# Sampled tokens of the state space part: small tiles, a gate and norm of their own, and other places for their eight steps

## The chip, the cores and the metric

The kernel runs on one core of a Trainium2 chip. Its time is device microseconds (us) of one execution, lower is better. Matrix products run on TensorE (PE), elementwise work on VectorE (DVE), ScalarE (ACT, which also evaluates functions) and GpSimd (POOL); SyncE (SP) issues nearly all DMAs, in one queue. All engines run their own instruction queues in order and wait for each other by semaphores.

## What is computed

One layer of a decoder for two groups of requests that share all weights: a prompt of 1024 positions, and 8 sampled tokens that continue from given states. Cut to what matters here:

```python
h = rmsnorm(x, w['norm1_w'])
proj = h @ w['w_in']
q_r, f_r, i_r, g_r, z, xbc_r, dt_r = jnp.split(proj, splits, axis=-1)
# group A: HGRN2 recurrence on q, f, i, g (8 heads of 128) -> o_a
xbc, buf_s_new = causal_dwconv(xbc_r, buf_s, w['ssm_conv_w'], w['ssm_conv_b'])
xbc = jax.nn.silu(xbc)
xs, Bm, Cm = jnp.split(xbc, [D_SSM, D_SSM + SSM_GROUPS * SSM_STATE], axis=-1)
y, S_s_new = ssd_scan(X * dt[..., None], A * dt, Bh, Ch, S_s)   # X: 16 heads of 64
y = y + w['ssm_d'][:, None] * X
y = y.reshape(Bsz, L, D_SSM) * jax.nn.silu(z)
y = rmsnorm(y.reshape(Bsz, L, SSM_GROUPS, -1), w['ssm_norm_w'].reshape(SSM_GROUPS, -1))
x = x + jnp.concatenate([o_a, y], axis=-1) @ w['w_out']
# then norm, gated MLP with a depthwise convolution, residual, final norm
```

For a sampled token the scan is one step: the state of each head is decayed by exp(A dt), the outer product of X dt and B is added, the product of the new state with C, summed over the 128 state columns, is y. The new states are outputs. Width of the state space part is 1024, in 2 groups of 512; all data are float32, and each operand of a large product is split into a high and a low part, so that it takes three matmuls.

## The kernel before, in words

Activations lie feature by token: a tile has 128 features as partitions and 1032 columns, 1024 prompt positions and then the 8 sampled tokens. The input projection is a list of jobs (`in_job`, L290), one for each 128 columns of `w_in`. A job makes three chunks of 344 columns, 72 matmuls in all, in three PSUM banks that rotate; after each chunk `evict` takes the bank over, on ACT. The jobs' order around the change is x0 to x3, x9, x11, x4 to x7 (the tiles of X; 8 to 11 are B and C), z0 to z3, f0, q0, v0, sg0 (head 0 of group A), z4 to z7, f1 and so on. A job's weights are fetched two jobs ahead (`wload`, L180) into two raw and two split buffers; `fetch` (L172) puts a DMA on SP's queue behind the last weight load that the program text had reached.

PE's order is written out by hand. `drive` (L266) runs a stream of larger work, such as the scan `ssd(g)` (L713) of group g, and between its pieces as many job steps (one matmul each) as keep both going; `ssd(0)` runs beside x9 to x7, `ssd(1)` beside z0 to v0, head 0 beside f1 to sg1. `after(n, work)` (L229) emits work n steps later. On the other engines a planner in the compiler orders the instructions, by their place in the program text and by when it believes them ready, so work of a later job may run earlier where its inputs and buffers are there.

`xbc_close` (L363) takes the convolution (four passes, `conv_tail`) and SiLU of one tile; L369 is the prompt's SiLU and L370 that of the sampled tokens, into columns 1024 to 1031 of the same tile. `ssd_front` (L530) and `ssd_back` (L560) do one chunk of 128 positions of the scan: L541/L542 the decays on ACT, L554/L557 the operands on DVE, L574, L580, L590, L593 outputs and state on DVE, L555/L579 on POOL.

`ssm_decode(g, i)` (L625) is one sampled-token step, for tile j = 4g + i (two heads, all 8 tokens). In two halves of 4 tokens it fetches B and C broadcast to 128 partitions and the states (tiles Bb, Cb in tag "d" with 4 buffers, Sd in tag "ld" with 2), decays the states on ACT (L638, four), multiplies B by X dt (L639) and adds (L640) on DVE, writes the state out (L641), multiplies by C on POOL (L642) and sums on DVE (L643); L629 and L644 frame it on 8 columns. It reads and writes columns 1024 to 1031 of X's tile. Its eight calls stand at the begin of x5, x7, z0 and z1 (group 0) and z4 to z7 (group 1).

`ssm_gate(g)` (L653) makes the gate: each z chunk goes through SiLU on ACT (L670, tile sz, tag "z" with 4 buffers), multiplies X in place on DVE (L671), is squared on ACT (L673/L675) and added up (L676). After the group's fourth job and 36 or 50 more steps, `rstd(c)` sums the squares over features with a matmul with ones (bank tag "nx", one buffer, which head 0's L834/L842 use too) and takes the reciprocal root (`rstd_of`, L646: one ACT, three DVE). `tail` then scales the four tiles on DVE (L694) and writes them to the scratch `mix_d`, from which the output projection reads them much later.

Of the kernel before, what the change touches and what calls it, by code (L numbers as in the profile page):

```python
# [8 lines left out]
F32 = mybir.dt.float32  # L9
F32R = mybir.dt.float32r  # L10
U8 = mybir.dt.uint8
AF = mybir.ActivationFunctionType
ALU = mybir.AluOpType
# [3 lines left out]
P = 128  # L17
DM = 1024
T = 1024
ND = 8  # L20
NT = T + ND
CH = 344
NCH = 3
# [27 lines left out]
def hybrid_layer(  # L51
# [9 lines left out]
    V, A, G, PE, SP = nc.vector, nc.scalar, nc.gpsimd, nc.tensor, nc.sync  # L61
# [9 lines left out]
    def nm(s):  # L71
        cnt[0] += 1
        return f"{s}_{cnt[0]}"
# [4 lines left out]
    const = part.enter_context(tc.tile_pool(name="const", bufs=1, side="right"))  # L78
    small = part.enter_context(tc.tile_pool(name="small", bufs=2, side="right"))
    tmp = part.enter_context(tc.tile_pool(name="tmp", bufs=1, side="right"))  # L80

    def tl(tag, name, dt=F32):
        w, n = TAGS[tag]
        return (work if tag in ("hT", "big", "e", "g") else tmp).tile([P, w], dt, tag=tag, bufs=n, name=nm(name))
# [4 lines left out]
    def bank(s, tag="mx"):  # L89
        return psmx.tile([P, 512], F32, tag=tag, bufs=NBANK[tag], name=nm(s))  # L90

    def mm(out, lhsT, rhs, start=True, stop=True):
        PE.matmul(out, lhsT, rhs, start=start, stop=stop)  # L93
# [55 lines left out]
    def col(name, i=0):  # L149
        c = vlay[name] + i  # L150
        return vcol[:, c:c + 1]
# [58 lines left out]
    chunks = [slice(c * CH, (c + 1) * CH) for c in range(NCH)]  # L210
# [18 lines left out]
    def after(n, work):  # L229

        later.append([n, work])
# [106 lines left out]
    Xg = [[None] * 4 for _ in range(2)]  # L338
    BT, CT, S = [None, None], [None, None], [None, None]
    last11 = const.tile([P, XT, 11], F32, name="last11")  # L340
    mix_d = dram.tile([16, P, NT], F32, name="mix_d")
    bc_d = dram.tile([4, ND, P], F32, name="bc_d")

    def conv_tail(acc, ext, nw, wname, bname, j, ntile, n):
        A.activation(acc[:, :n], ext[:, :n], AF.Identity, bias=col(bname, j), scale=col(wname, j))
        for q in range(1, nw):
            V.scalar_tensor_tensor(acc[:, :n], ext[:, q:q + n], col(wname, q * ntile + j), acc[:, :n],
                                   op0=ALU.mult, op1=ALU.add)

    def xbc_open():  # L350
        ext = tl("e", "ext")
        G.memset(ext[:, 0:3], 0.0)
        return ext

    def xbc_evict(j, ext, c, cs, ps):
        e = min(cs.stop, T)
        A.copy(ext[:, 3 + cs.start:3 + e], ps[:, :e - cs.start])
        if c == 2:
            V.tensor_copy(ext[:, 3 + T:3 + T + 32].rearrange("p (b r) -> p b r", r=4)[:, :, 3:4],
                          ps[:, T - cs.start:].unsqueeze(2))  # L360
            V.tensor_copy(last11[:, j, :], ps[:, CH - 11:])

    def xbc_close(j, ext):  # L363
        G.tensor_copy(ext[:, 3 + T:3 + T + 32].rearrange("p (b r) -> p b r", r=4)[:, :, 0:3],
                      bufT[:, j, :].rearrange("p (b r) -> p b r", r=3))
        n = T + 32
        acc = tl("big", "xbc")
        conv_tail(acc, ext, 4, "cw", "cb", j, XT, n)
        A.activation(acc[:, :T], acc[:, :T], AF.Silu)  # L369
        A.activation(acc[:, T:NT], acc[:, T + 3:T + 32:4], AF.Silu)  # L370
        return acc

    def xbc_job(j, put):
        ext = []
        def begin():
            ext.append(xbc_open())
            if j in (5, 7):
                ssm_decode(0, (5, 7).index(j))

        in_job(f"x{j}", OFF_X + j * P, lambda c, cs, ps: xbc_evict(j, ext[0], c, cs, ps), begin=begin, end=lambda: put(xbc_close(j, ext[0])))  # L380

# [20 lines left out]
    ones = keep.tile([P, P], F32, name="ones")  # L402
# [24 lines left out]
    for c, cs in enumerate(chunks):  # L427
        ps = psmm.tile([P, 512], F32, tag="mm", name=nm("dt"))
# [9 lines left out]
    for i in range(9):  # L438
        n = P if i < 8 else ND
# [171 lines left out]
    def d4(t):  # L611
        return t.rearrange("p (b n) -> p b n", n=P)
# [12 lines left out]
    def ssm_decode(g, i):  # L625
        j = g * 4 + i
        xdd = small.tile([P, 2, ND], F32, tag="xdd", name=nm("xdd"))
        xdec = Xg[g][i][:, T:NT]
        V.tensor_tensor(xdd[:, 0, :], xdec, ddb[:, 0, j, :], op=ALU.mult)  # L629
        for b0 in (0, 4):  # L630
            bs = slice(b0, b0 + 4)
            Bb, Cb = tl("d", "Bb")[:, :512], tl("d", "Cb")[:, :512]
            for t_, r in ((Bb, 2 * g), (Cb, 2 * g + 1)):
                fetch(t_, bc_d[r, bs].rearrange("b n -> (b n)").unsqueeze(0).to_broadcast([P, 512]))
            Sd = tl("ld", "Sd")
            fetch(d4(Sd), state_ssm[0, bs, 2 * j:2 * j + 2].rearrange("b h p n -> (h p) b n"))
            for b in range(4):
                A.activation(d4(Sd)[:, b, :], d4(Sd)[:, b, :], AF.Copy, scale=ddb[:, 1, j, b0 + b:b0 + b + 1])  # L638
            V.tensor_tensor(d4(Bb), d4(Bb), cb(xdd[:, 0, bs]), op=ALU.mult)  # L639
            V.tensor_tensor(Sd, Sd, Bb, op=ALU.add)  # L640
            SP.dma_start(ssm_sample[0, bs, 2 * j:2 * j + 2].rearrange("b h p n -> (h p) b n"), d4(Sd))  # L641
            G.tensor_tensor(Cb, Sd, Cb, op=ALU.mult)  # L642
            V.tensor_reduce(xdd[:, 1, bs], d4(Cb), axis=mybir.AxisListType.X, op=ALU.add)  # L643
        V.scalar_tensor_tensor(xdec, xdec, d_bc[:, j:j + 1], xdd[:, 1, :], op0=ALU.mult, op1=ALU.add)  # L644

    def rstd_of(dst, tmp, ps, n):  # L646

        A.activation(dst, ps, AF.Abs_reciprocal_sqrt, bias=epsc, scale=1.0 / n)
        V.scalar_tensor_tensor(tmp, ps, n * EPS, dst, op0=ALU.add, op1=ALU.mult)
        V.scalar_tensor_tensor(tmp, tmp, -0.5 / n, dst, op0=ALU.mult, op1=ALU.mult)  # L650
        V.scalar_tensor_tensor(dst, tmp, 1.5, dst, op0=ALU.add, op1=ALU.mult)

    def ssm_gate(g):  # L653
        acc = []

        def z_job(i):
            j = g * 4 + i

            def begin():
                if i == 0:  # L660
                    acc.append(tl("g", "gacc"))
                if g:
                    ssm_decode(1, i)
                elif i < 2:
                    ssm_decode(0, i + 2)

            def evict(c, cs, ps):
                Y = Xg[g][i][:, cs]
                sz = tl("z", "sz")[:, :CH]
                A.activation(sz, ps, AF.Silu)  # L670
                V.tensor_tensor(Y, Y, sz, op=ALU.mult)  # L671
                if i == 0:
                    A.activation(acc[0][:, cs], Y, AF.Square)  # L673
                else:
                    A.activation(sz, Y, AF.Square)  # L675
                    (V if g or i == 3 else G).tensor_tensor(acc[0][:, cs], acc[0][:, cs], sz, op=ALU.add)  # L676
                if i == 3:
                    after(36 + 14 * g, lambda: rstd(c))
            in_job(f"z{j}", OFF_Z + j * P, evict, begin=begin)

        def rstd(c):
            cs = chunks[c]
            ps = bank("ms", "nx")
            mm(ps[:, :CH], ones, acc[0][:, cs])
            rstd_of(acc[0][:, cs], tl("z", "nt")[:, :CH], ps[:, :CH], 512)

            if c == NCH - 1:
                tail()

        def tail():  # L690
            for i in range(4):
                j = g * 4 + i
                Y = Xg[g][i][:, :NT]
                V.scalar_tensor_tensor(Y, Y, col("sn", j), acc[0][:, :NT], op0=ALU.mult, op1=ALU.mult)  # L694
                SP.dma_start(mix_d[8 + j], Y)

        for i in range(4):
            z_job(i)
# [107 lines left out]
    def head_in(h):  # L806
        t = {}

        def f_end():
            f, k = t["f"], tl("big", "k")  # L810
            A.activation(f[:, :NT], f[:, :NT], AF.Identity, bias=lbt[:, 0, h:h + 1], scale=lbt[:, 1, h:h + 1])
            V.tensor_scalar(k[:, :NT], f[:, :NT], -1.0, 1.0, op0=ALU.mult, op1=ALU.add)
            t["k"] = k

        for n, off, func in (("f", OFF_F, AF.Sigmoid), ("q", OFF_Q, AF.Silu), ("v", OFF_I, AF.Copy),
                             ("sg", OFF_G, AF.Silu)):
            def evict(c, cs, ps, n=n, func=func):
                A.activation(t[n][:, cs], ps, func)

            def begin(n=n):  # L820
                t[n] = tl("e" if h == 0 and n == "f" else "big", n)

            if h == H - 1 and n == "sg":
                in_job_last(f"{n}{h}", off + h * P, evict, begin)
            else:
                in_job(f"{n}{h}", off + h * P, evict, begin, f_end if n == "f" else None)
        return t
# [539 lines left out]
    with tc.manual_schedule(engines={mybir.EngineType.PE}):  # L1367
# [56 lines left out]
        for r0 in range(0, FT - RND, RND):  # L1424
# [3 lines left out]
            for m in range(0, KT, 2):  # L1428
                wh, wl = wload(w_down[0, rows, m * P:(m + 2) * P], nk, 2 * P)
                for i in range(2):  # L1430
# [3 lines left out]
                    for c, cs in enumerate(quarters):  # L1434
                        ps = down(lambda k: (wh[:, k, :], wl[:, k, :]), nk, slice(i * P, (i + 1) * P), acts, c)
# [14 lines left out]
    for c in (3, 0, 1, 2):  # L1450
        cs = quarters[c]
        for m in range(KT):
            ps = down(lambda k: wd[k], nk, slice(m * P, (m + 1) * P), acts, c)
            V.tensor_tensor(xT[m][:, cs], xT[m][:, cs], ps, op=ALU.add)
        for t0 in range(cs.start, cs.stop, P):
            n = min(P, cs.stop - t0)
# [10 lines left out]
            for i in range(2):  # L1467
# [4 lines left out]
                else:  # L1472
                    V.scalar_tensor_tensor(ot[i][:n], tb[i][:n, :], ss[:n, 3:4], fw[:n, ds],  # L1473
                                           op0=ALU.mult, op1=ALU.mult)
# [31 lines left out]
```

## Time and profile before

| | us |
|---|---|
| median of 3 runs | 1765.55 (1763.43 to 1767.76) |
| profiled execution, its time | 1763.89 |
| profiled execution, its span | 1762.2 |
| PE busy | 1713.2 |
| DVE, ACT, POOL busy | 1105.4, 812.3, 482.0 |
| 128x512 elementwise product on DVE (L639), mean | 0.72 |
| the same size on POOL (L642), mean | 1.53 |
| matmul of a job, 344 columns, mean | 0.33 |

The profile is of one execution. Matmuls overlap in the pipeline, so their durations add up to more than PE's busy time. A row of a view that groups instructions reads: line, engine, operation, out<-in, shape, count | busy us in all, mean ns of one | the engine's idle us just before these instructions and what ended it. A row of the view of waits reads: who waited, for what: us in all, times, longest. A row of the view by windows reads: the stretch and its length, then busy us (count) of PE, weight loads, DVE, ACT and POOL, PE's granted clock (1.00 is full), the mean share of the DMA engines' time, GB/s. A row of the timeline reads: start, duration, engine, line, operation, count.

### The profile page before, as it was taken

To read this page: it belongs to the slowest core of one execution; us is meant where nothing else is said; L and a number is where in the kernel's file an instruction comes from. 1 tells how busy PE (TensorE), PEld (TensorE's weight loads), DVE (VectorE), ACT (ScalarE), POOL (GpSimd) and SP (SyncE) were. 2 spreads that over 40 slices of the span, in tenths; PEclk is the share of its full clock that TensorE was granted. 3 is DMA by queue.
4 is the path that set the end of the run, shared out by engine and by line. 5 is a ranking of instruction groups with operands and counts; after the bars stand their busy time and mean duration, and the time that the engine had idled before them with its cause. 6 is when DMAs were issued, how large, how long until landed. Compare 5 with 4: busy or idle time off the path is not lost. (4 is left out here: it accounts for less than half of the span.)

```text
span 1762.2 us, 38558 instructions
## 1 busy us (share of the span) xinstructions
PE 1713.2 (97%) x16111; PEld 1662.8 (94%) x16111; DVE 1105.4 (63%) x1988; ACT 812.3 (46%) x1450; POOL 482.0 (27%) x485
## 2 busy tenths in 40 slices
PE   7999899999999999999899999999999999999998
PEld 6999799998999999999799989999999999999997
DVE  6668966575554554466636688776667777445545
ACT  7577698454544454454423374334333434111114
POOL 2103332120110110112220355666666664000002
PEclk9999999999999999999899999999999999999999
DMA  5355744643321332234336742222222226422312
GB/s 166 68 147 155 189 117 136 179 139 105 88 89 51 98 87 80 69 115 143 110 113 212 245 127 73 73 85 85 85 73 73 80 78 217 152 85 78 98 61 97
DMA packets 249828, 199.17 MB, mean 113 GB/s; under 512 B 47212, under 2 KB 220822, under 8 KB 249638
## 3 DMA queue, kind: packets, MB, share of 16 engines
q1 hardware_dynamic: 249366, 196.61, 36.8%
q8 instruction: 126, 2.06, 0.5%
q14 instruction: 48, 0.39, 0.1%
q0 software_dynamic: 288, 0.10, 0.0%
HBM read 154.11 MB, written 46.94 MB: 114 GB/s over the span
## 5 line engine op out<-in xcount | busy, mean ns | idle before, releaser
L93 PE MATMUL mm<-hh,wh 128*128 128x344 f32 x1248 | 405.9, 326 | 2.0 <-issue 1.2
L93 PE MATMUL mm<-hl,wh 128*128 128x344 f32 x1248 | 405.5, 325 | 0.0
L93 PE MATMUL mm<-hh,wl 128*128 128x344 f32 x1248 | 402.4, 323 | 0.0
L93 PEld LDWEIGHTS mm<-hh,wh 128*128 128x128 f32 x1248 | 235.4, 189 | 6.5 <-issue 3.9
L93 PEld LDWEIGHTS mm<-hl,wh 128*128 128x128 f32 x1248 | 235.4, 189 | 4.5 <-issue 3.3
L93 PEld LDWEIGHTS mm<-hh,wl 128*128 128x128 f32 x1248 | 235.7, 189 | 1.8 <-issue 1.4
L190 ACT CAST wh<-ws 128x1024 fp32r<-128x1024 f32 x96 | 100.6, 1047 | 254.1 <-PE dn L93 135.0
L93 PE MATMUL ub<-uh,wh 128*128 128x258 f32 x704 | 199.3, 283 | 3.1 <-DVE fext L1319 2.7
L93 PE MATMUL ub<-ul,wh 128*128 128x258 f32 x704 | 199.0, 283 | 0.0
L93 PE MATMUL ub<-uh,wl 128*128 128x258 f32 x704 | 198.7, 282 | 0.0
L93 PE MATMUL dn<-ah,wh 128*128 128x256 f32 (+1 forms) x640 | 181.1, 283 | 2.0 <-DVE x L1436 2.0
L93 PE MATMUL dn<-al,wh 128*128 128x256 f32 (+1 forms) x640 | 180.6, 282 | 0.0
L93 PE MATMUL dn<-ah,wl 128*128 128x256 f32 (+1 forms) x640 | 180.1, 281 | 0.0
L192 DVE TENSOR_TENSOR wl<-ws,wh 128x1024 fp32r<-128x1024 f32 x88 | 108.7, 1235 | 75.7 <-ACT wh L190 68.6
L93 PE MATMUL mm<-mh,wh 128*128 128x258 f32 x512 | 148.2, 289 | 4.1 <-ACT x L1064 2.8
L93 PE MATMUL ua<-uh,wh 128*128 128x258 f32 x528 | 149.6, 283 | 1.3 <-DVE val L1331 1.3
L93 PE MATMUL ua<-ul,wh 128*128 128x258 f32 x528 | 149.3, 283 | 0.0
L93 PE MATMUL ua<-uh,wl 128*128 128x258 f32 x528 | 148.4, 281 | 0.0
L93 PE MATMUL mm<-ml,wh 128*128 128x258 f32 x512 | 146.9, 287 | 0.8 <-DVE ml L1024 0.8
L93 PE MATMUL mm<-mh,wl 128*128 128x258 f32 x512 | 146.5, 286 | 0.0
L93 PEld LDWEIGHTS ub<-uh,wh 128*128 128x128 f32 x704 | 132.9, 189 | 3.8 <-DVE fext L1319 2.9
L1269 DVE TENSOR_TENSOR wl<-wt,wh 128x512 fp32r<-128x512 f32 x88 | 89.6, 1037 | 74.2 <-ACT wh L1268 73.9
(351 smaller groups left out, 4037.2 us busy)
## 6 DMA issues: line engine op xcount, KB each, us to landing
ws<-in_w_in_dram SPq DMA_DIRECT2D x52, 512.0 KB
ws<-in_w_up_dram SPq DMA_DIRECT2D x44, 512.0 KB
ws<-in_w_out_dram SPq DMA_DIRECT2D x24, 512.0 KB
act_d<-val SPq DMA_DIRECT2D x22, 516.0 KB
al<-act_d SPq DMA_DIRECT2D x22, 516.0 KB
ws<-in_w_down_dram SPq DMA_DIRECT2D x22, 512.0 KB
ml<-mix_d SPq DMA_DIRECT2D x48, 172.0 KB
csb<-cs_d SPq DMA_DIRECT2D x32, 256.0 KB
```

The costliest lines, as they stand in the source:

```text
L93: PE.matmul(out, lhsT, rhs, start=start, stop=stop)
L190: A.copy(wh[:, :n], ws[:, :n])
L192: V.tensor_tensor(wl[:, :n], ws[:, :n], wh[:, :n].bitcast(F32), op=ALU.subtract)
L1269: V.tensor_tensor(lo[:, cs], sums[name], hi[:, cs].bitcast(F32), op=ALU.subtract)
```

## The change

The sampled tokens of X get a tile of their own, `xdk` (8 tiles of X by 8 tokens), written by `xbc_close`; `ssm_decode` works there. The gate's SiLU for these 8 columns is copied by POOL to `szd`, and the evictions, the sums of squares and the tail treat only the 1024 prompt positions (the last chunk has 336 columns). `decode_gate` and `decode_norm` do gate, norm and output for the four tiles of a group at once. The eight steps now stand at the begin of z3 (0,0), f0 (0,1), q0 (0,2), v0 (0,3), sg0 (1,0), z4 (1,1), z5 (1,2) and z6 (1,3). Group 0's gate follows 24 steps after v0 begins and its norm 20 steps later; group 1's gate follows 180 steps after its tail.

```diff
+    xdk = const.tile([P, 8, ND], F32, name="xdk")
+    szd = const.tile([P, 8, ND], F32, name="szd")
...
-        A.activation(acc[:, T:NT], acc[:, T + 3:T + 32:4], AF.Silu)
+        A.activation(xdk[:, j, :] if j < 8 else acc[:, T:NT], acc[:, T + 3:T + 32:4], AF.Silu)
...
-            if j in (5, 7):
-                ssm_decode(0, (5, 7).index(j))
...
-        xdec = Xg[g][i][:, T:NT]
+        xdec = xdk[:, j, :]
...
+        if j == 3:
+            after(24, lambda: decode_gate(0))
+
+    def decode_gate(g):
+        js = slice(4 * g, 4 * g + 4)
+        dg = small.tile([P, 6, ND], F32, tag="dg", bufs=1, name=nm("dg"))
+        V.tensor_tensor(xdk[:, js, :], xdk[:, js, :], szd[:, js, :], op=ALU.mult)
+        V.tensor_tensor(dg[:, 0:4, :], xdk[:, js, :], xdk[:, js, :], op=ALU.mult)
+        V.tensor_reduce(dg[:, 4, :], dg[:, 0:4, :].rearrange("p j b -> p b j"), axis=mybir.AxisListType.X, op=ALU.add)
+        after(20, lambda: decode_norm(g, js, dg))
+
+    def decode_norm(g, js, dg):
+        ps = bank("dgs", "nx")
+        mm(ps[:, :ND], ones, dg[:, 4, :])
+        rstd_of(dg[:, 4, :], dg[:, 5, :], ps[:, :ND], 512)
+        for j in range(js.start, js.stop):
+            V.scalar_tensor_tensor(xdk[:, j, :], xdk[:, j, :], col("sn", j), dg[:, 4, :], op0=ALU.mult, op1=ALU.mult)
+        SP.dma_start(mix_d[8 + js.start:8 + js.stop, :, T:NT].rearrange("j p b -> p j b"), xdk[:, js, :])
...
-                if g:
-                    ssm_decode(1, i)
-                elif i < 2:
-                    ssm_decode(0, i + 2)
+                if g and i < 3:
+                    ssm_decode(1, i + 1)
+                elif j == 3:
+                    ssm_decode(0, 0)
...
+                cs = slice(cs.start, min(cs.stop, T))
+                n = cs.stop - cs.start
...
+                if c == NCH - 1:
+                    G.tensor_copy(szd[:, j, :], sz[:, n:])
+                sz = sz[:, :n]
...
-                Y = Xg[g][i][:, :NT]
-                V.scalar_tensor_tensor(Y, Y, col("sn", j), acc[0][:, :NT], op0=ALU.mult, op1=ALU.mult)
-                SP.dma_start(mix_d[8 + j], Y)
+                Y = Xg[g][i][:, :T]
+                V.scalar_tensor_tensor(Y, Y, col("sn", j), acc[0][:, :T], op0=ALU.mult, op1=ALU.mult)
+                SP.dma_start(mix_d[8 + j][:, :T], Y)
+            if g:
+                after(180, lambda: decode_gate(1))
...
             def begin(n=n):
+                if h == 0:
+                    i = "fqvs".index(n[0])
+                    ssm_decode(*((0, i + 1) if i < 3 else (1, 0)))
```

More of the change, by code (lines that the diff above doesn't have):

```diff
@@ L681, in rstd @@
         def rstd(c):
-            cs = chunks[c]
+            cs = slice(chunks[c].start, min(chunks[c].stop, T))
+            n = cs.stop - cs.start
             ps = bank("ms", "nx")
-            mm(ps[:, :CH], ones, acc[0][:, cs])
-            rstd_of(acc[0][:, cs], tl("z", "nt")[:, :CH], ps[:, :CH], 512)
+            mm(ps[:, :n], ones, acc[0][:, cs])
+            rstd_of(acc[0][:, cs], tl("z", "nt")[:, :n], ps[:, :n], 512)
             if c == NCH - 1:
```

## The prediction

> **What bounds the kernel now.** I read the page first, for the engine that is never free.
>
> ```profile
> span 1762.2 us, 38558 instructions
> ...
> PE 1713.2 (97%) x16111; PEld 1662.8 (94%) x16111; DVE 1105.4 (63%) x1988; ACT 812.3 (46%) x1450; POOL 482.0 (27%) x485
> ```
>
> TensorE (PE) is busy 1713.2 of 1762.2 us, and the change leaves its matmuls alone but for two products with 8 columns. So the only thing to win is its idle time, 49 us in all, and the part of that which lies where sampled-token steps run. The second view is what PE waited for between 136 us (job x4) and 425 us (head 0), the stretch that the diff touches.
>
> ```profile
> PE yo L93 <- DVE S L580: 3.1, 1, 3.1
> PE a L93 <- DVE q L873: 2.8, 1, 2.8
> PE ms L93 <- DVE vd L842: 1.4, 1, 1.4
> PE yd L93 <- DVE xdt L554: 1.4, 2, 1.0
> PE mm L93 <- ACT sz L670: 0.8, 1, 0.8
> ```
>
> These are the five longest, and all but one are for VectorE (DVE). The third view cuts the stretch by stages: x4 and x5; x6 and x7; z0 to z2; z3 to q0; v0 and sg0; z4 to z7; the start of head 0. Columns are busy us of PE, weight loads, DVE, ScalarE (ACT), GpSimd (POOL), then PE's granted clock and the DMA share.
>
> ```profile
> 136.00:172.00 36.00, 36.00 (x264) 32.27 (x263) 31.64 (x54) 28.71 (x62) 12.26 (x11) 1.00 0.65 171
> 172.00:213.00 41.00, 35.92 (x243) 31.46 (x240) 39.63 (x65) 25.68 (x58) 13.39 (x13) 0.96 0.69 178
> 213.00:259.00 46.00, 46.00 (x314) 43.60 (x312) 30.94 (x54) 40.65 (x81) 17.11 (x13) 1.00 0.47 124
> 259.00:309.00 50.00, 49.74 (x346) 45.47 (x346) 36.13 (x66) 42.41 (x73) 10.44 (x9) 1.00 0.45 138
> 309.00:339.00 30.00, 30.00 (x208) 28.12 (x207) 18.00 (x32) 13.30 (x29) 4.82 (x4) 1.00 0.59 176
> 339.00:384.00 45.00, 42.81 (x271) 41.97 (x270) 25.72 (x46) 19.40 (x48) 7.70 (x6) 1.00 0.56 164
> 384.00:420.00 36.00, 32.72 (x582) 30.98 (x582) 29.26 (x44) 23.58 (x34) 5.04 (x4) 0.95 0.36 119
> 200.00:210.00 10.00, 6.86 (x41) 5.02 (x40) 10.00 (x15) 3.30 (x8) 2.35 (x2) 0.83 0.64 167
> 410.00:420.00 10.00, 9.55 (x186) 9.18 (x173) 5.14 (x9) 5.12 (x11) 0.00 (x0) 0.83 0.17 50
> ```
>
> From 172 to 213 us DVE is busy 39.63 of 41 us and PE stands 41.00 - 35.92 = 5.1 us. There DVE is the bound, and nowhere else in the stretch. Behind the longest wait the granted clock is 0.83 for 10 us, which is another 10 x 0.17 = 1.7 us. So this one place costs 6.8 us.
>
> **The change part by part.** *The steps leave x5, x7, z0 and z1.* These groups are one step's work, eight times:
>
> ```profile
> L640 DVE TENSOR_TENSOR Sd<-Sd,Bb 128x512 f32<-128x512 f32 x16 | 12.6, 788 | 0.5 <-ACT Sd L638 0.3
> L639 DVE TENSOR_TENSOR Bb<-Bb,xdd 128x512 f32<-128x512 f32 x16 | 11.5, 718 | 16.1 <-DMA Bb<-bc_d 16.1
> L643 DVE TENSOR_REDUCE xdd<-Cb 128x4 f32<-128x512 f32 x16 | 10.9, 683 | 15.3 <-POOL Cb L642 15.3
> L644 DVE SCALAR_TENSOR_TENSOR xbc<-xbc,d_bc,xdd 128x8 f32<-128x8 f32 x8 | 1.8, 220 | 0.1
> L629 DVE TENSOR_TENSOR xdd<-xbc,ddb 128x8 f32<-128x8 f32 x8 | 1.3, 164 | 5.4 <-DMA ddb<-dd_d 5.3
> L638 ACT ACTIVATE Sd<-Sd,ddb 128x128 f32<-128x128 f32 x64 | 20.9, 394 | 14.0 <-DMA Sd<-in_state_ssm_dram 7.8 <-DMA Cb<-bc_d 5.3 <-issue 0.9
> L642 POOL TENSOR_TENSOR Cb<-Sd,Cb 128x512 f32<-128x512 f32 x16 | 24.4, 1526 | 68.7 <-DVE Sd L640 55.3 <-DMA csb<-cs_d 9.0 <-DMA Cb<-bc_d 4.4
> ```
>
> DVE: (12.6 + 11.5 + 10.9 + 1.8 + 1.3) / 8 = 4.8 us a step; ACT 2.6; POOL 3.1; and eight DMAs on SP's queue (four Bb and Cb, two states in, two out). DVE also stood (16.1 + 15.3) / 8 = 3.9 us a step before L639 and L643, where its queue had come to a step whose data or POOL product was not there. Between 136 and 213 us lie nearly three steps, 14 us of DVE's 71.3 (31.64 + 39.63). Without them DVE has 57 us to do in what would be 77 - 6.8 = 70 us: 81%, under the 88% (31.64 of 36) at which PE lost nothing between 136 and 172. The operations that PE waits for at 172 to 213 are ordinary ones late in DVE's queue:
>
> ```profile
> 204.12 0.67 DVE L580 TENSOR_TENSOR S<-S,st 128x512 f32<-128x512 f32 x1
> 206.38 2.14 DVE L593 SCALAR_TENSOR_TENSOR xbc<-xbc,d_bc,ecs 128x128 f32<-128x128 f32 x4
> 210.97 1.13 DVE L593 SCALAR_TENSOR_TENSOR xbc<-xbc,d_bc,ecs 128x128 f32<-128x128 f32 x4
> ...
> 206.54 1.31 POOL L642 TENSOR_TENSOR Cb<-Sd,Cb 128x512 f32<-128x512 f32 x1 [0.62 <-DVE Sd L640]
> ```
>
> L580 would be some 14 us earlier in DVE's queue, against 3.1 us of wait, so what is late next is PE itself. Bounds: 0 to -6.8; I take all, **-6.8 us**. The steps can't drift back there: their fetches stand behind the weight load of the job after theirs, and f0's weights are asked for only after z0 has ended (two buffers each for raw and split weights).
>
> *z7 has no step, and a step's end no longer stands before an eviction.* In z4 to z7 the step writes columns 1024 to 1031 of X before the third eviction may multiply them. The last backlog of this ends here:
>
> ```profile
> 383.41 0.27 DVE L842 COPY vd<-vd 8x128 f32<-8x128 f32 x1
> ```
>
> PE stood 1.4 us for that copy, behind z7's evictions. With no step in z7 I take **-1.4** (bounds 0 and -1.4). The 0.8 us wait for an eviction at z5 or z6 stays: steps still run there. Head 0's wait (2.8 us, and 1.7 us of clock by the last row of the stages) is for an operation behind the tail of group 1, which stays: 0, with -4.5 as the other end.
>
> *The steps arrive beside z3, f0, q0, v0, sg0.* Steps start early (below), so about three of them fall between 259 and 309 us: DVE 36.1 + 3 x 4.8 = 50.5 of 50 us, ACT 42.4 + 3 x 2.6 = 50.2 of 50. That is as full as 172 to 213 was. What speaks for a small price: 213 to 259 gives up the rest of two old steps, and from 309 to 339 DVE has 12 us free and ACT 17, into which a late step may slip, since now nothing but the norm waits for it. Bounds: 0 (as 136 to 172) and +6.8 (the old stall whole); I take **+1.5**, nearer the first, for this room.
>
> *Transfers.* Some 2 MB a step leave a stage with DMA share 0.69 for stages with 0.45 to 0.59. SP now stands at a step's state output among csb, ecs and weight loads of these jobs.
>
> ```profile
> SPq L641 <- DVE Sd L640: 34.9, 15, 7.7
> ```
>
> That is 2.3 us a time, as before but elsewhere; weights are asked for two jobs ahead, so 0. The two small outputs to mix_d are read only in the output projection, hundreds of us later.
>
> *New small work.* Per group: a product, a square, a reduction, three operations of the reciprocal root, four scalings, one ACT root, one matmul; and eight POOL copies of 128x8.
>
> ```profile
> L649 DVE SCALAR_TENSOR_TENSOR od<-dms,od 128x8 f32<-128x8 f32 x8 | 1.3, 167 | 6.3 <-ACT od L648 6.3
> L648 ACT ACTIVATE od<-dms,epsc 128x8 f32<-128x8 f32 x8 | 2.1, 268 | 0.1
> L648 ACT ACT_TABLE_LOAD x20 | 25.7, 1283 | 0.4
> L1328 POOL COPY last<-fext 128x8 f32<-128x8 f32 x22 | 4.1, 187 | 0.0
> ```
>
> DVE 10 x 0.2 = 2 us a group, ACT 0.3 and at most two table loads of 1.3, POOL 8 x 0.2 = 1.5 us. Group 0's stands in v0 and group 1's in sg1, where DVE and ACT have room: 0; uncovered it is 2 us each. A POOL copy behind an L642 keeps one of four sz buffers longer; ACT's next eviction would wait, PE only after three banks: 0. The norm's matmul is a new wait in PE's own queue, with all of v0 behind it. It is put 44 of v0's 72 steps in:
>
> ```profile
> 224.82 0.46 ACT L670 ACTIVATE sz<-mm 128x344 f32<-128x344 f32 x1
> 235.04 0.22 DVE L644 SCALAR_TENSOR_TENSOR xbc<-xbc,d_bc,xdd 128x8 f32<-128x8 f32 x1
> ...
> L639 DVE TENSOR_TENSOR Bb<-Bb,xdd x16: 678/692/1155, 127.1 to 363.7; 128x512 f32<-128x512 f32 x16
> ```
>
> The latest step of before ended at 235.26, 10.4 us after z0's last eviction, its job's start. The first began L639 at 127.1, 25 us ahead of its job x5: the planner pulls steps forward. A job beside the SSD takes about 16 us, so 44 steps are 9.8 us. Bounds: 0 and 10.4 + 0.6 (the gate) - 9.8 = 1.2, with 1.7 of clock 2.9; I take 0, since v0's fetches may go as soon as sg0's weights are asked for, after the end of z3, two jobs ahead.
>
> **Sum:** -6.8 - 1.4 + 1.5 = -6.7. The profiled execution took 1763.89 us (span 1762.2 and 1.7 around it), so 1757.2; the median of the runs, 1765.55, lies 1.66 above it. Forecast **1758.9**; its own range is 1756 to 1763.
>
> On the clock: the gap of 3.1 us at 205 and that of 2.8 at 410 both show 0.83 behind them. The Trainium skill (TensorE: Matmul & The Clock Gate, Why this matters for your kernels) says that idle gaps over about 3 us bring the half clock. By that rule the second gap would be free; the trace disagrees slightly, and the sum, in which only the first gap goes, is the same by both.
>
> **Rivals.** (a) *Head 0 catches up too*: DVE enters it without backlog, and the waits 0.8, 2.8 and 1.7 of clock go as well: -6.8 - 1.4 - 5.3 = -13.5, 1752.1. For it: DVE is busy 29.26 of 36 us there, behind z7's backlog; against: the tail of group 1 is still ahead of what PE awaits. Chance 0.14.
>
> (b) *The stall only moves*: z3 to q0 becomes what x6 and x7 were: -1.4 in all, 1764.2. For it: 50.5 of 50 us; against: the room behind. Chance 0.21.
>
> (c) *The queue waits come along, slower*: a step's price in order is 4.8 + 3.9 = 8.7 us of DVE, since its queue stands before L639 and L643. DVE has 50 - 36.1 = 13.9 us idle between 259 and 309; n steps lose 8.7n - 13.9 and win 8.2. Break-even is n = 2.5, slower by over 0.3% from n = 3.2; at 3.5 it is +8.4, 1774.0. For it: steps pulled forward bunch there. Against: the mean of 3.9 includes z4 to z7, where DVE is busy only 25.72 of 45 us and its idle time goes down as a wait for whatever comes next. Chance 0.12.
>
> The Trainium skill (SBUF — State Buffer, SBUF: two separate sides) says that GpSimd and a two-input DVE operation lock each other out of a shared port. The trace agrees: L593 took 2.14 us beside POOL's L642 and 1.13 without. By that rule three steps would add up to 3 x 3.1 us to DVE there, which speaks for (c); in my sum it is inside the measured means.
>
> (d) *The norm's matmul waits*: +2.9, 1761.8. Chance 0.05.
>
> **Chances.** Forecast 0.48, (a) 0.14, (b) 0.21, (c) 0.12, (d) 0.05. A measurement of this kernel tells about 0.3% (5.3 us) from no change, so faster means under 1760.25. Of the forecast's 0.48, 0.36 lies there, and all of (a): 0.50. Same: the other 0.12, (b), (d) = 0.38. Slower: 0.12. The range goes from 1750 to 1771 and leaves out most of (c) and the end of (a).
>
> **What will show it.** Right: no PE wait for L580 or L554 in x6 and x7, no granted clock under 1 there, DVE near 81%; no wait for L842; L639 from about 230 us on. Wrong: new PE waits for L580, xdt, or sz evictions between 230 and 310 us (b, c), DVE idle before L639 there (c), a wait of the new norm's matmul in v0 (d), or the x6 to x7 waits standing although DVE has room, which would mean a chain through ACT and not DVE's load.

## The result and the profile after

The changed kernel takes 1767.89 us (median of 19 runs, 1763.22 to 1773.74) against 1764.71 us for 19 runs of the kernel before beside it. The ratio is 1.0017, with a 95% interval of 1.0010 to 1.0025: some 3 us slower, where 6.7 us faster was forecast. The time lies within 0.3% of before and inside the widest range that the prediction gives (1750 to 1771 us), but outside that of its forecast (1756 to 1763 us), and the change moved it the other way.

The page of the changed kernel shows TensorE as busy as before and the span 3.0 us longer.

```profile
span 1765.2 us, 38611 instructions
...
PE 1711.8 (97%) x16115; PEld 1662.8 (94%) x16115; DVE 1112.3 (63%) x2008; ACT 811.2 (46%) x1451; POOL 486.2 (28%) x493
```

These are the longest waits of PE in the changed kernel, 136 to 425 us.

```profile
PE dgs L93 <- DVE dg L654: 6.0, 1, 6.0
PE ms L93 <- DVE gacc L700: 4.3, 1, 4.3
PE a L93 <- DVE q L903: 2.8, 1, 2.8
```

Of the waits that the prediction wanted gone (S, xdt, vd) none is left, and the one for sz, which it expected to stay, is gone too. Two others are there in their place: the new norm's matmul (dgs) and the older sum of squares of z3 (ms). The stages of the changed kernel, same stretches and columns as before, show where they lie:

```profile
172.00:213.00 41.00, 41.00 (x288) 38.11 (x289) 33.71 (x54) 26.73 (x51) 7.59 (x7) 1.00 0.46 122
...
259.00:309.00 50.00, 45.39 (x302) 41.21 (x301) 41.87 (x76) 43.04 (x80) 14.71 (x11) 0.97 0.67 203
309.00:339.00 30.00, 23.97 (x151) 21.81 (x150) 23.76 (x49) 12.06 (x29) 9.31 (x8) 0.89 0.76 202
339.00:384.00 45.00, 45.00 (x287) 45.00 (x286) 24.87 (x41) 19.42 (x46) 9.27 (x8) 1.00 0.57 163
384.00:420.00 36.00, 32.99 (x557) 31.42 (x556) 29.43 (x49) 23.01 (x33) 5.94 (x5) 0.95 0.36 118
```

Against the rows of before, idle time and lost clock together: 172 to 213 us wins 5.1 + 0.04 x 41 = 6.7; 339 to 384 wins 2.2; the start of head 0 wins 0.3. 259 to 309 loses 4.4 + 0.03 x 50 = 5.9, and 309 to 339 loses 6.0 + 0.11 x 30 = 9.3. That is +6.0. Equal stretches of time do not hold quite the same work in both kernels, so one and the same matmul is the better measure. This one, in head 1, starts 4.1 us later than in the kernel before (first row: before, second row: after):

```profile
443.63 0.64 PE L93 MATMUL hms<-sq,ones 128*32 128x256 f32 x8
447.75 0.64 PE L93 MATMUL hms<-sq,ones 128*32 128x256 f32 x8
```

Followed in this way, PE gains 7.5 us up to 211 us, loses 6.0 by 305 and 8.9 more by 318, and wins back 2.6 up to the end of z7 and 0.5 in head 0. So the rows have the two losses nearly right and the gains too small. Behind the heads the lag falls to 1.3 us at 862 us and ends at 2.7 from 1563 us on, beside a measured +3.0 of span. From 836 to 880 us no step runs; the granted clock was 0.88 there in the profiled execution of before and 0.96 in that of the changed kernel, which alone makes 0.08 x 44 = 3.5 us. Over the profiled executions of all eleven kernels it was between 0.84 and 0.96 there.

**Why the norm waited.** The timeline of the changed kernel, from the second state of step (0,2) to the norm (in brackets the engine's idle time before the operation and what ended it):

```profile
264.88 0.39 SPq L175 DMA_DIRECT2D Sd<-in_state_ssm_dram  x1
...
266.46 0.49 ACT L699 ACTIVATE sz<-xbc 128x344 f32<-128x344 f32 x1 [2.27 <-DVE xbc L695]
...
273.91 0.38 SPq L189 DMA_DIRECT2D ws<-in_w_in_dram  x1
...
286.08 1.56 ACT L639 ACTIVATE Sd<-Sd,ddb 128x128 f32<-128x128 f32 x5
...
300.78 0.38 SPq L175 DMA_DIRECT2D Sd<-in_state_ssm_dram  x1
...
318.54 0.22 DVE L645 SCALAR_TENSOR_TENSOR xdk<-xdk,d_bc,xdd 128x8 f32<-128x8 f32 x1
...
319.92 0.60 PE L93 MATMUL dgs<-dg,ones 128*128 128x8 f32 x2 [6.03 <-DVE dg L654]
...
320.56 0.27 ACT L667 ACTIVATE dg<-dgs,epsc 128x8 f32<-128x8 f32 x1 [7.23 <-PE dgs L93]
321.90 0.46 ACT L845 ACTIVATE v<-mm 128x344 f32<-128x344 f32 x1 [1.08 <-PE mm L93]
```

Step (0,2)'s states were asked for by 264.9 us, but their decay on ACT (L639) began at 286.1, behind 20 us of other ACT work without a gap, and DVE came to the additions behind it (L641) only at 294.5. So the buffers came free late. The row at 273.91 is the fetch of sg0's weights (the twentieth of w_in, behind those of 12 x jobs, z0 to z3, f0, q0 and v0): from there on the program text lets (0,3)'s fetches go, as the prediction had it. But (0,3)'s first state was asked for only at 300.8, and the step's end (L645) came at 318.5. PE had come to the norm's matmul 6.0 us before it could run. ACT, in order too, stood 7.23 us at the norm's root; v0's eviction behind it (L845) then waited 1.08 us more, for PE's matmul, so it was PE's stop that held it and not ACT's.

**Why z3's sum of squares waited.** The same view, just ahead of the end of PE's wait for gacc at 263.87 us:

```profile
260.08 0.51 DVE L695 TENSOR_TENSOR xbc<-xbc,sz 128x344 f32<-128x344 f32 x1
260.51 0.68 DVE L641 TENSOR_TENSOR Sd<-Sd,Bb 128x512 f32<-128x512 f32 x1
262.71 0.69 DVE L644 TENSOR_REDUCE xdd<-Cb 128x4 f32<-128x512 f32 x1 [1.52 <-POOL Cb L643]
263.31 0.51 DVE L700 TENSOR_TENSOR gacc<-gacc,sz 128x344 f32<-128x344 f32 x1
...
260.80 0.47 ACT L699 ACTIVATE sz<-xbc 128x344 f32<-128x344 f32 x1
```

The square that L700 adds was there at 261.3. Ahead of L700 in DVE's queue stand step (0,1)'s L641 and L644, and before L644 DVE did nothing for 1.52 us, because POOL's product of that step was not there. Earlier the step had been in the way on ACT too: eight of its decays (L639, 255.0 to 257.4 us) ran just ahead of the eviction of z3 (L691, at 257.4) from which this sum is made.

### The profile page after: what moved, and what is told of

Its sections match the earlier page's. It is cut to its first block, busy times and chain, and to the rows that moved or that the text cites. A ratio compares the mean times of both kernels' runs of the same rounds, so it can differ in the third digit from the quotient of the medians.

```text
span 1765.2 us, 38611 instructions
## 1 busy us (share of the span) xinstructions
PE 1711.8 (97%) x16115; PEld 1662.8 (94%) x16115; DVE 1112.3 (63%) x2008; ACT 811.2 (46%) x1451; POOL 486.2 (28%) x493
## 5 line engine op out<-in xcount | busy, mean ns | idle before, releaser
L1299 DVE TENSOR_TENSOR wl<-wt,wh 128x512 fp32r<-128x512 f32 x88 | 88.4, 1024 | 76.2 <-ACT wh L1298 76.2
```

What stands on the lines that cost most here:

```text
L1299: V.tensor_tensor(lo[:, cs], sums[name], hi[:, cs].bitcast(F32), op=ALU.subtract)
```

## The experiments

My theory was that two orderings cost the time: (1a) the norm's matmul stands too early in PE's queue, since ACT, full beside z3 and f0, holds up the steps; (1b) step operations stand ahead of z3's gating in DVE's queue. The rival was that DVE and ACT have too much to do in this stretch whatever the order, so that PE, freed of one wait, meets the next late operation. Line numbers of the kernels that follow differ by a few.

**The norm 72 steps later, in sg0.**

```diff
-        after(20, lambda: decode_norm(g, js, dg))
+        after(20 if g else 92, lambda: decode_norm(g, js, dg))
```

> The changed kernel, with group 0's norm matmul 92 instead of 20 steps after its gate, so in sg0 instead of v0. Theory 1 (the norm's matmul stands in PE's queue before its sum is ready: 6.0 us of wait and 6.8 us at half clock, 3.4 us lost): the wait goes, about 9 us less than the changed kernel, ratio to before 0.996 to 0.998. Rival 2 (PE has no slack there, since DVE and ACT are full from z2 to v0; the wait only hides one that comes behind it, for S, yo or an eviction): at most 3 us less, ratio 1.000 to 1.002.

Measured: 0.9993 (0.9984 to 1.0002) of before. PE's waits, 136 to 425 us:

```profile
PE ms L93 <- DVE gacc L700: 3.8, 1, 3.8
...
PE mm L93 <- ACT sz L691: 2.5, 3, 1.4
PE sT L606 <- DVE S L581: 0.7, 1, 0.7
```

The 6.0 us wait is gone, and 309 to 339 us has full clock. But a part comes back as waits for sz (2.5) and S (0.7), and the ratio falls by 0.0024, 4.2 us, where the wait and its clock had cost 9.3 by the rows. So (1a) holds for the place of the wait, and the rival for some of its price.

**The small tiles alone, steps at their old places.** The calls of `ssm_decode` go back to x5, x7, z0, z1 and z4 to z7, and both gates follow 180 steps behind their tails.

> Small tiles, gate and norm of their own as changed, but the eight steps at their old places (x5, x7, z0, z1, z4 to z7); group 0's gate follows its tail by 180 steps as group 1's does. Theory 1 (the moved steps alone change the waits at x6 and x7): the waits of before for S and xdt there come back, 5 us and a half clock, and there is no wait of the norm's matmul and none of 4 us for gacc; ratio 0.999 to 1.000. If the small tiles (a step no longer stands before an eviction) and not the empty z7 removed the waits for vd (1.4) and sz (0.8), both are gone here too; if the empty z7 did it, both are back. Rival 2 (the small tiles themselves cost, by POOL's copies and the gates): ratio over 1.001.

Measured: 1.0005 (0.9994 to 1.0015). The old waits are all back:

```profile
PE yo L93 <- DVE S L583: 3.1, 1, 3.1
...
PE mm L93 <- ACT sz L691: 1.9, 1, 1.9
PE ms L93 <- DVE vd L868: 1.7, 1, 1.7
```

So the tiles, the gate and the norm cost nothing that can be measured and win nothing either; all that the change does to the time comes from the places of the steps and of the norm that waits for them. It also corrects a reason of mine: the waits for sz and vd went with the places of the steps (the changed kernel has none in z7), not because an eviction no longer has to wait for a step's end, since that freedom is here too.

**The decay taken from ACT.**

```diff
-            for b in range(4):
-                A.activation(d4(Sd)[:, b, :], d4(Sd)[:, b, :], AF.Copy, scale=ddb[:, 1, j, b0 + b:b0 + b + 1])
+            G.tensor_tensor(d4(Sd), d4(Sd), cb(ddb[:, 1, j, bs]), op=ALU.mult)
```

> The changed kernel, with the states' decay of each step as one POOL product of 128x512 in place of four ACT operations (ACT loses 2.6 us a step, POOL gains about 2 times 1.3). Theory 1a (step (0,2) stood from 268 to 294 us because ACT was full in z3 and f0, and so (0,3) and the norm came late): (0,2) and (0,3) end earlier by some 10 us or more, the norm's matmul waits under 2 us, ratio about 0.997 to 0.999. Rival (the step was late through SP's queue, buffers or DVE): (0,3) ends as late as before and the norm's matmul waits 5 us or more, ratio 1.001 or over.

Measured: 1.0069 (1.0053 to 1.0084), the slower way. The timeline of this kernel:

```profile
269.30 1.04 POOL L638 TENSOR_TENSOR Sd<-Sd,ddb 128x512 f32<-128x512 f32 x1 [8.19 <-DMA Sd<-in_state_ssm_dram]
...
271.29 1.49 POOL L580 TENSOR_TENSOR S<-S,etot 128x512 f32<-128x512 f32 x1
...
270.37 1.51 DVE L640 TENSOR_TENSOR Sd<-Sd,Bb 128x512 f32<-128x512 f32 x1 [2.58 <-POOL Sd L638]
271.81 1.35 DVE L694 TENSOR_TENSOR xbc<-xbc,sz 128x344 f32<-128x344 f32 x1
273.08 1.77 DVE L639 TENSOR_TENSOR Bb<-Bb,xdd 128x512 f32<-128x512 f32 x1
```

Step (0,2) decays its state at 269.3 instead of 286.1 us, as soon as the state is there, and it ends at 288.8 instead of 299.4: ACT was what held this step up. (0,3), whose fetches here go right behind sg0's weights, gains less: it ends at 314.1 instead of 318.5. That PE waits for dgs no more proves nothing by itself, since other waits bring PE to that matmul 10 us later here (324.1 instead of 313.9 us). PE now waits 6.5 us for the root of z3 (ms), 4.0 for S and 2.9 for ecs. Beside POOL's products DVE's own take 1.51, 1.35 and 1.77 us; the first two are the L641 and L695 shown above for the changed kernel, 0.68 and 0.51 us with POOL idle beside them. The Trainium skill (SBUF — State Buffer, SBUF: two separate sides) has GpSimd and two-input DVE operations lock each other out of a shared port; the trace agrees with these numbers.

**Two steps back to z0 and z1, the norm late.** (0,0) stands at z0, (0,1) at z1; z3 and f0 have none.

> As the first of these (norm in sg0), with the steps of group 0 at z0, z1, q0 and v0 in place of z3, f0, q0 and v0, so that no step stands in z3 and f0, where ACT is fullest. Theory 1b (the wait of 4.3 us and its half clock for gacc in z3 comes from the operations of a step ahead of it in DVE's queue): that wait goes too, 4 to 6 us less than the first, ratio 0.993 to 0.995. Rival (steps pulled forward into x7 to z1 bring back the waits for S of before): a wait for S at x7 or z0 of 2 us or more, ratio 0.997 or over.

Measured: 1.0012 (1.0001 to 1.0023).

```profile
PE sT L606 <- DVE S L581: 3.1, 2, 2.4
PE mm L93 <- ACT sz L691: 2.9, 2, 2.7
```

The wait for gacc is gone, so the steps at z3 and f0 made it (1b). Waits for S are back at 200 and 207 us (0.9 and 2.4), with steps that start there, and one of 2.7 for sz at 368 us comes besides. Moving two steps up by a few jobs only exchanges one wait for others.

**z3's sum of squares later too.** The norm late, and

```diff
-                    after(36 + 14 * g, lambda: rstd(c))
+                    after(66 - 16 * g, lambda: rstd(c))
```

> As the kernel with the late norm, and group 0's three matmuls of the root stand 66 instead of 36 steps behind the evictions that they follow. Theory 1 (the wait of 3.8 to 4.3 us in z3 is the same thing as the norm's: a matmul put in PE's queue before its sum is ready): it goes, with its half clock, 3 to 6 us under the late norm, ratio 0.996 to 0.998. Rival (PE then meets the next late operation of DVE, since the steps have DVE full there): a wait for S, xdt or an eviction of 2 us or more between 250 and 320 us, ratio 0.999 or over.

Measured: 1.0011 (1.0002 to 1.0019). PE no longer waits for gacc, but longer for the root made from it, and then for S:

```profile
PE ms L93 <- DVE nt L668: 5.2, 1, 5.2
...
PE sT L606 <- DVE S L581: 2.6, 1, 2.6
```

Here (1b) falls as a remedy: the step operations do make the wait, but a later place of the matmul only passes it on. The rival is right about the time, and the wait for S that it expected comes at 326 us.

**No steps at all.** The kernel leaves out the step bodies, so its time is about the floor for this question (about, since the planner orders the rest anew).

> The changed kernel with the body of all eight steps left out (no state update, no output of the states, the gate works on X itself): what the steps cost PE in the changed kernel. Theory 1: no wait of the norm's matmul, none for gacc in z3, none for S; what is left from 136 to 425 us is head 0's 2.8 us; ratio 0.993 to 0.995. Rival 2 (the stretch is bound by DVE and ACT even without steps, by table loads and the gate's chain): waits of 4 us or more stay between 136 and 390 us, ratio 0.997 or over.

Measured: 0.9943 (0.9929 to 0.9956). PE's longest wait from 136 to 425 us is head 0's, 2.6 us, so without steps DVE and ACT do keep up there. The eight steps cost the changed kernel 1.0017 - 0.9943 = 0.0074, 13 us, though no engine but PE is full over the whole span.

**The steps into the heads.** They stand at v0, sg0 and sg1 to sg6, one beside each head; the gate follows 24 steps behind a group's fourth step and the norm 92 steps later. Only with tiles of their own can they go there: X's tiles are scaled and written by the tail long before.

```diff
-                if h == 0:
-                    i = "fqvs".index(n[0])
-                    ssm_decode(*((0, i + 1) if i < 3 else (1, 0)))
+                if h == 0 and n == "v":
+                    ssm_decode(0, 0)
+                if n == "sg" and h < 7:
+                    ssm_decode((h + 1) // 4, (h + 1) % 4)
```

> Small tiles as changed, but the eight steps at v0, sg0 and then one in each of sg1 to sg6, where DVE, ACT and POOL have most room; each group's gate 24 steps after its last step begins, its norm 92 after that. Theory 1 (a step costs PE time only where DVE and ACT are full, x6 to f0 and z4 to z7): the waits for S at x6 and x7, for gacc in z3, for sz and vd in z4 to z7 all go and nothing comes in the heads but some tenths: 8 to 11 us under the kernel before, ratio 0.994 to 0.996. Rival (a step costs PE the same wherever it stands, through waits at the head of DVE's queue and the shared buffers of the heads' states): new waits of 1 us or so in each head, ratio 0.998 or over.

Measured: 0.9978 (0.9968 to 0.9988), faster than both kernels. What is left between 136 and 425 us:

```profile
PE sT L606 <- DVE xdd L630: 3.2, 1, 3.2
PE a L93 <- DVE q L898: 2.7, 1, 2.7
```

The first stands beside the two steps of v0 and sg0, which the planner ran at 276 to 318 us; the operation named is the first of step (0,2), the last that DVE did before PE went on, while sT needs S, which DVE had updated just ahead of it, behind the end of (0,1). Between 410 and 735 us, where the other six run, PE has a single wait over 0.5 us, of 0.8.

**All eight in jobs of heads 1 to 4, two to a head** (at v1, sg1 to v4, sg4).

> All eight steps stand at v and sg of heads 1 to 4, none beside z3 to z6 or in head 0; gates and norms follow 24 and 92 steps behind the fourth step of a group. Theory (a step costs nothing where VectorE, ScalarE and GpSimd have room, and what it costs is the wait of an ordinary operation in a full stage): the wait of 3.25 us for xdd at 319 us and the half clock behind it (1.7 us), which the steps of v0 and sg0 made, go, no other comes, and the ratio to before falls from 0.9978 to 0.995, near the 0.9943 of the kernel without steps; the heads' excess between 460 and 800 us stays within 2 us of 22. Rival (each step has a price of its own wherever it stands, some 0.8 us, as 6.2 us between the kernel with steps in the heads and the one without steps, over eight steps, would have it): 0.998 again, with new waits in heads 1 to 4, where two steps now lie beside each head.

Measured: 1.0062 (1.0046 to 1.0078), a miss by both accounts. PE waits in the heads now, 6.3 us the longest. This is the largest group; another, 4.4 us in two waits, is for the root of a head's norm (od):

```profile
PE a L93 <- DVE q L897: 9.1, 3, 6.3
```

Its timeline in head 1:

```profile
451.22 0.43 SPq L175 DMA_DIRECT2D Bb<-bc_d  x1
458.15 3.07 SPq L879 DMA_DIRECT2D out_dram<-Sh  x2
...
461.87 0.40 SPq L175 DMA_DIRECT2D Bb<-bc_d  x1
...
466.78 0.69 DVE L640 TENSOR_TENSOR Bb<-Bb,xdd 128x512 f32<-128x512 f32 x1 [7.11 <-DMA Cb<-bc_d]
...
468.92 0.67 DVE L897 TENSOR_TENSOR q<-q,tt 128x512 f32<-128x512 f32 x1
```

SP's queue had issued the first half's B and then stood at a head's state output (L879) until 458.2 us, with the second half's B behind it. DVE had come to that half's product and stood 7.11 us for it (the row names C, fetched in the same burst; the product reads B), with the head's own L897, for which PE waits, behind. DVE has room there (152.92 of 260 us from 460 to 720), so the shortage is not one of time. In all, DVE stood 29.8 us before these products in eleven waits, at the steps of v and of sg alike. What costs, where the trace was followed, is a step whose data is late when DVE's queue comes to it, with an operation behind it that PE needs.

**Two steps beside z4 and z6, six at sg1 to sg6.**

```diff
+                if g and i % 2 == 0:
+                    ssm_decode(0, i // 2)
...
-                if h == 0 and n == "v":
-                    ssm_decode(0, 0)
-                if n == "sg" and h < 7:
+                if n == "sg" and 1 <= h <= 6:
```

> Steps (0,0) and (0,1) stand at z4 and z6, the other six at sg1 to sg6, one beside each head; none beside z3 to sg0. Gates and norms follow 24 and 92 steps behind the fourth step of a group. Theory (what counts is whether the step's DMA is there when VectorE's queue comes to its product; one step beside a head is free, as in the kernel with the steps in the heads, and two are not, as in the kernel with all in heads 1 to 4, where VectorE stood 7.11 us for the second half's broadcast B): the wait for xdd at 319 us goes, z4 to z7 stay without an sz wait as after the change with three steps there, 460 to 800 us stays at an excess of 22 us: ratio 0.9955 (0.9945 to 0.9965). Rival 1 (each step costs 0.8 us wherever it stands): 0.998. Rival 2 (the sz and vd waits of z4 to z7 come back with steps there): waits of 0.8 and 1.4 us at 365 to 385 us and a ratio of 0.997.

Measured: 0.9944 (0.9930 to 0.9957), 1756.63 against 1765.84 us: the best of all, and, within the intervals, equal to the kernel without steps. Its stages:

```profile
259.00:309.00 50.00, 49.15 (x342) 44.52 (x341) 35.10 (x66) 40.17 (x70) 10.97 (x10) 1.00 0.41 122
...
384.00:420.00 36.00, 32.73 (x498) 31.37 (x497) 25.93 (x38) 20.46 (x37) 4.86 (x4) 1.00 0.48 160
```

PE loses 0.85 us from 259 to 309 and no clock at all, and in head 1 its timeline has a step's fetches one after the other behind the state output, not around it:

```profile
450.33 3.21 SPq L880 DMA_DIRECT2D out_dram<-Sh  x2
...
458.21 0.57 SPq L175 DMA_DIRECT2D Bb<-bc_d  x1
...
459.29 0.43 SPq L175 DMA_DIRECT2D Bb<-bc_d  x1
```

The planner ran the steps of z4 and z6 early, at 312 to 325 and 336 to 347 us. DVE stood 8.0 us before their products too, in four waits for B, but PE waited for nothing there: late data costs only where something that PE needs stands behind it. So steps at these places cost nothing that can be measured, and some 0.0074 / 8 of the time, 1.6 us, at the change's places on the mean.

## Why the prediction was wrong

**Right.** The stall at x6 and x7 went whole, clock and all (forecast -6.8, measured -6.7 by the rows and -7.5 by the same matmul), and nothing took its place there: from 136 to 213 us DVE is busy 29.12 + 33.71 = 62.83 of 77 us, 82% where 81% was worked out. The copy of vd is awaited no more (-1.4), though of the two reasons given for it one was wrong: a step's end before an eviction was not the cause. Head 0's wait stayed (2.8). The small operations cost nothing: the kernel with the small tiles alone differs from before by less than its interval. Nor did PE wait for a transfer in the stretch: none of its waits names one.

**Too careful.** "The 0.8 us wait for an eviction at z5 or z6 stays": it went as well; with the steps back in z4 to z7 it was 1.9.

**The step that failed: the norm's matmul**, "I take 0, since v0's fetches may go as soon as sg0's weights are asked for", bounds 0 and 2.9. It cost 6.0 us of wait and 3.3 of clock. I bounded it by the latest step of before, 10.4 us behind its job's start; there the two decays came 5 and 13 us after their states were asked for. In the new stage it was 24 us for step (0,2) (261.7 to 286.1), behind ACT's other work, against 7 with the decay on POOL, and the buffers hand that lateness on to the next step: its fetches could go at 273.9 us, as I had written, and went at 299.8 and later. I had written down that ACT would have 50.2 of 50 us to do there and drew from it only the general price of the stage, not the lateness of the steps themselves, on whose end the one new wait hung. Rival (d) names this place, at less than a third of its price, and got a chance of 0.05.

**The term that was too small: the arrival beside z3 to q0**, +1.5 within 0 to +6.8. The stage lost 4.4 us of PE's time, nearly all in the one wait of 4.3, and 1.5 by its clock: 5.9, near the upper end. The room behind, from 309 us on, does not help an operation that stands in the queue ahead of z3's gating, and it was filled too: DVE is busy 23.76 of 30 us there, not 18. Rival (b), the stall that only moves, describes this half.

Put right by the rows, the sum is -6.7 - 2.2 - 0.3 + 5.9 + 9.3 = +6.0; by the same matmul it is -7.5 - 2.6 - 0.5 + 6.0 + 8.9 = +4.3, of which the rest of the kernel, where no step runs, gives some back. Rival (c), DVE's queue standing at steps whose data is late, did not come: DVE stood 17.6 us in all before the groups of L640 and L644 (7.5 and 10.1), where before it was 31.4. It has a part in both new waits (1.52 us ahead of z3's sum, 0.79 and 0.78 before the last reductions ahead of the norm), and the kernel with two steps to a head shows it in full.

That the norm's wait is a part of the loss is shown by taking it away: 4.2 us come back. That the steps at z3 and f0 make the other wait is shown too, since it goes with them; but the time did not fall in either kernel that removed it, so its price is read from the rows and not shown by a run. That no removal there wins its whole price fits a stretch from x6 to sg0 without room on DVE and ACT; this is argued from the waits for sz, S and nt that follow, and from the two kernels that reach 0.994 with no step beside z3 to q0. What is not settled is which of these later waits follows from which: the planner orders DVE, ACT and POOL anew for every kernel.

## What to carry to other kernels

When a side job is moved, work out its own latency at the new place, engine by engine, before putting a matmul that needs its end into the queue of the engine that bounds the kernel: a busy share for a stage doesn't say how long one operation stands behind others. When a wait is only passed on from place to place, the stretch is full; take the work out of it, and compare with a kernel that leaves it out, which tells what there is to win. A job in an idle stretch can still cost: when an in-order queue comes to it before its data is there, everything behind it waits, and that is paid for where the bounding engine needs one of the things behind. One step to a head stayed clear of this here, two did not.

## What the runs showed of the hardware

In these executions the granted clock behind a gap is not settled by the gap's length alone. Head 0's wait was 2.8 us in the changed kernel, with a clock of 0.95 for 384 to 420 us, and as long in the last kernel, with 1.00:

```profile
PE a L93 <- DVE q L898: 2.8, 1, 2.8
```

The Trainium skill (TensorE: Matmul & The Clock Gate, Why this matters for your kernels) puts the bound at gaps of about 3 us; these runs show both outcomes just under it. Such a difference is 0.05 x 36 = 1.8 us of 1760, so a profiled span alone can't judge a change of that size.

ACT spent more on loading its function tables than on any group of its work in the full stage, 259 to 309 us of the changed kernel. The table loads of that window, and its largest group of work (L542):

```profile
L542 ACT ACTIVATE csb<-csb,cst 128x128 f32<-128x128 f32 x28 | 9.0, 389 | 0.0
L543 ACT ACT_TABLE_LOAD x5 | 6.4, 1283 | 0.0
L667 ACT ACT_TABLE_LOAD x3 | 3.8, 1283 | 0.1
L845 ACT ACT_TABLE_LOAD x3 | 3.8, 1283 | 0.1
...
L691 ACT ACT_TABLE_LOAD x2 | 2.6, 1283 | 0.0
```

The loads are 16.6 of ACT's 43.04 us, since the scan's exponentials, z's SiLU, the roots and the head's evictions take turns there.
